# Second group's first load on the scalar queue, and other cuts of the first group's stores

## The chip, the cores and the metric

The kernel runs on one core of a Trainium2 chip. The metric is the device time of one execution in microseconds (us). The core has, among others, VectorE (DVE in the profile, does all the products here), ScalarE (ACT, two activations and some transfers) and SyncE (SP, only issues transfers). Data moves between HBM (the device's memory) and SBUF (the on-chip memory of 128 partitions) by 16 DMA engines. A transfer is issued by an engine's queue: those of SyncE are named q1 in the profile, those of ScalarE q10. Each transfer here covers 128 partitions, and its data go as one packet for each partition, so 8 packets on each of the 16 DMA engines.

## The reference

```python
def setup_inputs():
    batch, seq, hidden, n_experts, k = 16, 1024, 512, 8, 2
    ...
def reference(x, router_logits, k):
    logits_max = np.max(router_logits, axis=-1, keepdims=True)
    probs = np.exp(router_logits - logits_max)
    probs = probs / np.sum(probs, axis=-1, keepdims=True)
    topk_indices = np.argsort(probs, axis=-1)[..., -k:]
    topk_probs = np.take_along_axis(probs, topk_indices, axis=-1)
    topk_probs = topk_probs / np.sum(topk_probs, axis=-1, keepdims=True)
    x_expanded = x[:, :, np.newaxis, :].repeat(k, axis=2)
    return (x_expanded * topk_probs[..., np.newaxis]).astype(np.float32)
```

For each of 16,384 tokens (x is 16 x 1024 x 512, float32) the two largest of 8 router logits give two weights, and the token's 512 values are written twice, once times each weight. So 33.6 MB of x and 0.5 MB of logits are read, and 67.1 MB of output written.

## The kernel before, in words

Every partition holds 128 tokens, called rows here: 65 in a first group and 63 in a second (GROUPS). A row is 2 KB of x and 4 KB of output. The tile `xs` has room for 65 rows of x in each partition, and both groups use it; the second group's rows stand one place higher in it (BASE). The tile `osp` has room for L rows of output. Before that it serves as room for the logits and the steps of the search for the two largest (lines 14 to 38), which ends with two activations on ScalarE that leave the weights in `WA`.

For each group the kernel issues the loads of LOADS (line 120), 6, 28 and 31 rows in the first group and 16, 16 and 31 in the second, and then goes through the group's entries of STORES. An entry is (first row, number of rows, tile, place): VectorE multiplies these rows by their two weights (line 133) and puts the products into `osp`, or into `xs` itself over rows that are no longer needed (a product takes twice the room of its row), and then the store is issued (line 145). A product that writes again over `osp` from its start is made in two instructions (FREE): a few rows first, whose place was stored long ago, and the rest when the store of the place behind them has landed.

All transfers keep the program's order on their queue. All go over SyncE's queue, but for the very first store (3 rows), which goes over ScalarE's. A queue's transfers run one behind the other on the DMA engines. A load of the second group has to wait until the products that stand in its place in `xs` have been stored: the first 16 rows (places 1 to 16) for the first group's third store, out of places 0 to 31; the last 31 rows (places 33 to 63) for the fifth, out of places 33 to 64.

The order on SyncE is thus: load 6 rows, both parts of the logits, load 28, load 31; stores two to five of the first group; loads 16, 16 and 31 of the second; its four stores. In the text the stores of a group are counted with the one on ScalarE as the first.

Of the kernel before, what the change touches and what calls it, by code (L numbers as in the profile page):

```python
# [1 line left out]

# [4 lines left out]

F32 = mybir.dt.float32
ALU = mybir.AluOpType
ACTF = mybir.ActivationFunctionType  # L10
P = 128


def top2_weights(nc, WA, dlt, room, logits, E):

    tt = nc.vector.tensor_tensor
    hi, lo, n = None, None, E  # L20
    while n > 1:
        n //= 2
        if hi is None:
            a, b = logits[:, :, 0:n], logits[:, :, n : 2 * n]
            nhi, nlo = room(n), b
            tt(nhi, a, b, op=ALU.max)  # L26
            tt(nlo, a, b, op=ALU.min)  # L27
        else:
            a, b = hi[:, :, 0:n], hi[:, :, n : 2 * n]
            nhi, nlo, tmp = room(n), room(n), room(n)  # L30
            tt(tmp, lo[:, :, 0:n], lo[:, :, n : 2 * n], op=ALU.max)  # L31
            tt(nlo, a, b, op=ALU.min)  # L32
            tt(nlo, nlo, tmp, op=ALU.max)  # L33
            tt(nhi, a, b, op=ALU.max)  # L34
        hi, lo = nhi, nlo
    tt(dlt, hi[:, :, 0], lo[:, :, 0], op=ALU.subtract)  # L36
    nc.scalar.activation(WA[:, :, 0], dlt, ACTF.Sigmoid, scale=-1.0)  # L37
    nc.scalar.activation(WA[:, :, 1], dlt, ACTF.Sigmoid, scale=1.0)  # L38

GROUPS = [65, 63]

LOADS = [[6, 28, 31], [16, 16, 31]]
BASE = [0, 1]

STORES = [
    [(0, 3, "osp", 0), (3, 15, "osp", 3), (18, 16, "xs", 0), (34, 15, "osp", 0), (49, 16, "xs", 33)],
    [(0, 16, "osp", 2), (16, 16, "xs", 0), (32, 15, "osp", 0), (47, 16, "xs", 32)],
]  # L50

L = 18

FREE = [3, 2]


@with_exitstack
def kernel(
    ctx: ExitStack,
    tc: tile.TileContext,  # L60
    x: bass.AP,
    router_logits: bass.AP,
    k: bass.AP,
    out: bass.AP,
):
    nc = tc.nc
    B, S, D = x.shape
    E = router_logits.shape[-1]
    N = B * S
    assert int(k) == 2 and E == 8 and N == P * sum(GROUPS)  # L70
    M = N // P

    x_v, o_v, rl_v = [], [], []
    t0 = 0
    for n in GROUPS:
        t1 = t0 + P * n
        x_v.append(
            x.rearrange("b s d -> (b s) d")[t0:t1].rearrange("(p m) d -> p m d", p=P)
        )
        o_v.append(  # L80
            out.rearrange("b s k d -> (b s) k d")[t0:t1].rearrange(
                "(p m) k d -> p m k d", p=P
            )
        )
        rl_v.append(
            router_logits.rearrange("b s e -> (b s) e")[t0:t1].rearrange(
                "(p m) e -> p m e", p=P
            )
        )
        t0 = t1  # L90

    wpool = ctx.enter_context(tc.tile_pool(name="wpool", bufs=1))
    xs = wpool.tile([P, max(GROUPS), D], F32)
    osp = wpool.tile([P, L, 2, D], F32)
    WA = wpool.tile([P, M, 2], F32)
    dlt = wpool.tile([P, M], F32)


    flat = osp.rearrange("p l k d -> p (l k d)")
    taken = [0]  # L100

    def room(n):
        o = taken[0]
        taken[0] += M * n
        return flat[:, o : o + M * n].rearrange("p (m n) -> p m n", n=n)

    logits = room(E)

    def place(where, at, n):

        if where == "osp":
            return osp[:, at : at + n]
        return xs[:, at : at + 2 * n, :].rearrange("p (r k) d -> p r k d", k=2)

    m0 = 0
    for g, G in enumerate(GROUPS):
        x0, r = BASE[g], 0
        for n in LOADS[g]:
            tc.keep_in_program_order(
                nc.sync.dma_start(xs[:, x0 + r : x0 + r + n, :], x_v[g][:, r : r + n, :])  # L120
            )
            r += n
            if g == 0 and r == 6:
                n0 = GROUPS[0]
                tc.keep_in_program_order(nc.sync.dma_start(logits[:, :n0], rl_v[0]))  # L125
                tc.keep_in_program_order(nc.sync.dma_start(logits[:, n0:], rl_v[1]))  # L126
                top2_weights(nc, WA, dlt, room, logits, E)
        assert r == G
        for r, n, where, at in STORES[g]:
            og = place(where, at, n)  # L130
            again = where == "osp" and at == 0 and r > 0
            for a, b in [(0, FREE[g]), (FREE[g], n)] if again else [(0, n)]:
                nc.vector.tensor_tensor(  # L133
                    og[:, a:b],
                    xs[:, x0 + r + a : x0 + r + b, :]
                    .unsqueeze(2)
                    .to_broadcast([P, b - a, 2, D]),
                    WA[:, m0 + r + a : m0 + r + b, :]
                    .unsqueeze(3)
                    .to_broadcast([P, b - a, 2, D]),  # L140
                    op=ALU.mult,
                )

            queue = nc.scalar if g == r == 0 else nc.sync
            tc.keep_in_program_order(queue.dma_start(o_v[g][:, r : r + n], og))  # L145
        m0 += G


# [1 line left out]
_INS = ['x', 'router_logits', 'k']  # L150
_OUTS = [((16, 1024, 2, 512), 'float32')]

_NUMBERS = {'k': 2}


# [26 lines left out]
```

## Time and profile before

| | |
|---|---|
| median of 3 runs | 239.92 us (239.89 to 240.08) |
| profiled execution | 239.92 us, of which the profile's span is 238.1 us |
| VectorE busy | 141.9 us, 60% of the span |
| ScalarE busy | 1.8 us |
| moved by DMA | 101.19 MB, 425 GB/s over the span |
| products of 16 rows (128x16384) | 17.22 us each |
| product of 15 rows (128x15360) | 16.16 us |
| products of 13, 12, 3 and 2 rows | 14.03, 12.96, 3.35, 2.28 us |

The profile shows one execution. Its busy view cuts the span into 40 equal slices with a digit for the busy tenths of each; the DMA line there is the mean of 16 engines, and a long packet counts in the slice in which it begins, so that neighbouring digits go up and down. The queue view gives for each queue packets, megabytes and the share of 16 engines' time that the packets took. For a short window that share can exceed 100%, since packets that begin in the window count whole. The chain of waits goes back from the last instruction through whatever released each step; a transfer stands there from its issue to its landing, its wait in the queue included.

### The profile page before, as it was taken

The numbers are of one execution on the slowest core, as the hardware profiler recorded it, in microseconds if no ns is written. First come the engines' busy times: TensorE is split into PE (matmuls) and PEld (weight loads), VectorE is DVE, ScalarE is ACT, GpSimd is POOL, SyncE is SP. The second block draws the span as 40 slices with busy tenths as digits, with TensorE's granted clock in tenths as the row PEclk, the third lists the DMA queues.
The fourth block names the chain that finished last, engine by engine and source line by source line (L and its number), as shares of the span: only waits on it lengthen the run. The fifth ranks groups of instructions, "written<-read, shape, count | busy, mean of one in ns | idle before, by whom it ended". The sixth has DMA issues, their size and how long they took to land.

```text
span 238.1 us, 102 instructions
## 1 busy us (share of the span) xinstructions
DVE 141.9 (60%) x22; ACT 1.8 (1%) x3; POOL 0.2 (0%) x4
## 2 busy tenths in 40 slices
DVE  0650499999699999100000699999406999950000
ACT  2000000000000000000000000000000000000000
POOL 0000000000000000000000000000000000000000
DMA  7979998979999999989899999898989999989894
GB/s 265 550 337 500 430 418 374 506 330 495 429 429 407 473 423 402 495 352 528 352 440 435 435 446 501 352 495 374 506 374 462 418 407 451 475 351 517 352 528 176
DMA packets 2448, 101.19 MB, mean 425 GB/s; under 512 B 272, under 2 KB 400, under 8 KB 528
## 3 DMA queue, kind: packets, MB, share of 16 engines
q1 hardware_dynamic: 2304, 99.62, 97.2%
q10 hardware_dynamic: 144, 1.57, 1.5%
HBM read 34.08 MB, written 67.11 MB: 425 GB/s over the span
## 4 chain that ended last, share of the span: by engine, by line
DMA 48%; DVE 40%; SPq 1%; issue 0%; DVEq 0%
DMA xs<-in_x_dram 26%; DVE osp L133 25%; DMA out_dram<-osp 22%; DVE xs L133 14%; SPq L125 0%; SPq L126 0%; SPq L120 0%; SPq L145 0%; DVEq L133 0%
## 5 line engine op out<-in xcount | busy, mean ns | idle before, releaser
L133 DVE TENSOR_TENSOR osp<-xs,WA 128x3072 f32<-128x3072 f32 (+5 forms) x7 | 69.4, 9908 | 61.6 <-DMA xs<-in_x_dram 47.5
L133 DVE TENSOR_TENSOR xs<-xs,WA 128x16384 f32<-128x16384 f32 x4 | 68.9, 17224 | 0.1
L26 DVE TENSOR_TENSOR osp<-osp 128x512 f32<-128x512 f32 x1 | 0.7, 692 | 8.1 <-DMA osp<-in_router_logits_dram 8.1
L37 ACT ACT_TABLE_LOAD x1 | 1.3, 1283 | 0.7 <-PEq L163 0.7
L27 DVE TENSOR_TENSOR osp<-osp 128x512 f32<-128x512 f32 x1 | 0.7, 691 | 0.0
L34 DVE TENSOR_TENSOR osp<-osp 128x256 f32<-128x256 f32 (+1 forms) x2 | 0.7, 352 | 0.0
L32 DVE TENSOR_TENSOR osp<-osp 128x256 f32<-128x256 f32 (+1 forms) x2 | 0.7, 352 | 0.0
L31 DVE TENSOR_TENSOR osp<-osp 128x256 f32<-128x256 f32 (+1 forms) x2 | 0.7, 352 | 0.0
L33 DVE TENSOR_TENSOR osp<-osp 128x256 f32<-128x256 f32 (+1 forms) x2 | 0.7, 351 | 0.0
L37 ACT ACTIVATE WA<-dlt 128x128 f32<-128x128 f32 x1 | 0.3, 314 | 10.1 <-DVE dlt L36 10.1
L36 DVE TENSOR_TENSOR dlt<-osp 128x128 f32<-128x128 f32 x1 | 0.3, 291 | 0.0
L38 ACT ACTIVATE WA<-dlt 128x128 f32<-128x128 f32 x1 | 0.3, 298 | 0.0
L163 POOL MEMSET const-bfloat16-1.0<- 128x1 bf16 x1 | 0.1, 101 | 0.0
L163 POOL MEMSET const-uint8-127<- 128x1 uint8 x1 | 0.1, 101 | 0.0
L163 POOL MEMSET const-float32-0.0<- 128x1 f32 x1 | 0.1, 98 | 0.2 <-issue 0.2
L163 POOL MEMSET const-float32-1.0<- 128x1 f32 x1 | 0.1, 98 | 0.0
## 6 DMA issues: line engine op xcount, KB each, us to landing
out_dram<-osp SPq DMA_DIRECT2D x3, 7680.0 KB, 23.4
xs<-in_x_dram SPq DMA_DIRECT2D x2, 7936.0 KB, 41.7
xs<-in_x_dram SPq DMA_DIRECT2D x2, 4096.0 KB, 40.4
xs<-in_x_dram SPq DMA_DIRECT2D x1, 7168.0 KB, 24.8
xs<-in_x_dram SPq DMA_DIRECT2D x1, 1536.0 KB, 6.0
out_dram<-osp ACTq DMA_DIRECT2D x1, 1536.0 KB, 24.8
osp<-in_router_logits_dram SPq DMA_DIRECT2D x1, 260.0 KB, 6.2
osp<-in_router_logits_dram SPq DMA_DIRECT2D x1, 252.0 KB, 6.4
```

Of the source, the lines that this page charges most:

```text
L26: tt(nhi, a, b, op=ALU.max)
L27: tt(nlo, a, b, op=ALU.min)
L31: tt(tmp, lo[:, :, 0:n], lo[:, :, n : 2 * n], op=ALU.max)
L32: tt(nlo, a, b, op=ALU.min)
L33: tt(nlo, nlo, tmp, op=ALU.max)
L34: tt(nhi, a, b, op=ALU.max)
L36: tt(dlt, hi[:, :, 0], lo[:, :, 0], op=ALU.subtract)
L37: nc.scalar.activation(WA[:, :, 0], dlt, ACTF.Sigmoid, scale=-1.0)
L38: nc.scalar.activation(WA[:, :, 1], dlt, ACTF.Sigmoid, scale=1.0)
L133: nc.vector.tensor_tensor(og[:, a:b], xs[:, x0 + r + a : x0 + r + b, :] .unsqueeze(2) .to_broadcast([P, b - a, 2, D]), WA[:, m0 + r + a : ...
L163: nc = _bacc.Bacc("TRN2", target_bir_lowering=False, num_devices=1)
```

## The change

The first group's stores are cut to 3, 16, 16, 16 and 14 rows; they were 3, 15, 16, 15 and 16. `osp` gets 19 places for rows instead of 18. The second group's first load (16 rows) is issued by ScalarE's queue; it was SyncE's. An added dependency makes it wait until the first group's fourth store has landed. So it is issued while the fifth, now of 14 rows, is on SyncE's queue. The second group's middle load stays on SyncE's queue, directly behind that fifth store. Which engine makes which product, and in which order, is as before.

```diff
 STORES = [
-    [(0, 3, "osp", 0), (3, 15, "osp", 3), (18, 16, "xs", 0), (34, 15, "osp", 0), (49, 16, "xs", 33)],
+    [(0, 3, "osp", 0), (3, 16, "osp", 3), (19, 16, "xs", 0), (35, 16, "osp", 0), (51, 14, "xs", 37)],
     [(0, 16, "osp", 2), (16, 16, "xs", 0), (32, 15, "osp", 0), (47, 16, "xs", 32)],
 ]
 
-L = 18
+L = 19
...
     m0 = 0
+    stores = []
     for g, G in enumerate(GROUPS):
         x0, r = BASE[g], 0
         for n in LOADS[g]:
-            tc.keep_in_program_order(
-                nc.sync.dma_start(xs[:, x0 + r : x0 + r + n, :], x_v[g][:, r : r + n, :])
-            )
+
+            queue = nc.scalar if g == 1 and r == 0 else nc.sync
+            load = queue.dma_start(xs[:, x0 + r : x0 + r + n, :], x_v[g][:, r : r + n, :])
+            if queue is nc.scalar:
+                tc.add_manual_dep(
+                    load.ins,
+                    stores[-2].ins.name,
+                    mybir.DependencyInfo(
+                        mybir.DependencyClass.Sync, mybir.DependencyReason.DATA
+                    ),
+                    reason="begin when the store ahead of the last has landed",
+                )
+            tc.keep_in_program_order(load)
             r += n
...
             queue = nc.scalar if g == r == 0 else nc.sync
-            tc.keep_in_program_order(queue.dma_start(o_v[g][:, r : r + n], og))
+            stores.append(queue.dma_start(o_v[g][:, r : r + n], og))
+            tc.keep_in_program_order(stores[-1])
         m0 += G
```

## Prediction, made before the changed kernel was run

> **What bounds the kernel now.** I read the busy slices first, then the DMA queues, the chain of waits, and the transfers one by one by window. Busy slices and queues:
>
> ```profile
> DVE  0650499999699999100000699999406999950000
> DMA  7979998979999999989899999898989999989894
> ...
> HBM read 34.08 MB, written 67.11 MB: 425 GB/s over the span
> ...
> q1 hardware_dynamic: 2304, 99.62, 97.2%
> q10 hardware_dynamic: 144, 1.57, 1.5%
> ```
>
> VectorE has idle stretches of many slices; the DMA engines have none. q1 is SyncE's queue, q10 ScalarE's: their packets fill 97.2% + 1.5% = 98.7% of 16 engines over 238.1 us, 235.0 us each. The 3.1 us left are the head (0.72 us to the first issue, about 1 us more to its first packets) and the tail behind the last packets. So I look only for what makes a DMA engine idle or slow. The chain agrees, if one knows that a transfer's time in it includes its wait in the queue:
>
> ```profile
> by line: DMA xs<-in_x_dram 25.5%; DVE osp L133 25.4%; DMA out_dram<-osp 22.4%; DVE xs L133 14.5%; issue 0.2%; SPq L125 0.2%; SPq L126 0.2%; SPq L120 0.2%; SPq L145 0.1%; DVEq L133 0.0%
> ...
> 43.09 22.91 DMA out_dram<-osp
> ...
> 96.66 36.05 DMA xs<-in_x_dram
> ...
> 150.05 30.49 DMA out_dram<-osp
> ```
>
> The store issued at 43.09 lands at 66.00, but the load ahead of it on SyncE landed only at 47.85 (issued 2.60, 45.3 us to landing): its own data took 18.15 us for 7.86 MB, 433 GB/s. With issue plus time to landing from the DMA view, every later transfer begins where the one ahead ends. Landings: first group's stores 2 to 5 at 66.0, 85.3, 103.4, 123.0; second group's loads at 132.7, 142.4, 161.2; its stores at 180.5, 199.8, 218.0, 237.3. A 16-row store takes 19.3 us (66.0 to 85.3), a 16-row load 9.7 us (132.7 to 142.4). No stretch is empty.
>
> What two queues cost when they run together, the scalar queue's first store shows (issued at 16.00, between two SyncE loads). The DMA views of four windows: 7.70 to 17.72 (before it), 17.72 to 18.25 (just behind the issue), 23.12 to 23.60 (its second row has gone out) and 26.56 to 29.35 (well in), with packets, MB and share of 16 engines:
>
> ```profile
> q1 hardware_dynamic: 64, 3.67, 84.5%
> ...
> q1 hardware_dynamic: 16, 0.92, 433.2%
> ...
> q1 hardware_dynamic: 16, 0.92, 522.3%
> ...
> q1 hardware_dynamic: 16, 1.02, 83.9%
> q10 hardware_dynamic: 16, 0.20, 16.5%
> ```
>
> A share times 16 engines times the window, by packets, is one packet's time (it may end behind the window). Alone, a 57,344-byte load packet takes 0.845 x 16 x 10.02 / 64 = 2.12 us. The one that began between 17.72 and 18.25 (433.2% of 0.53 us) took 2.30 us, 0.18 more; the one begun at 23.1, the last of its load, 2.51 us, 0.39 more. After that both queues go in turn, one packet of each, and fill 83.9% + 16.5% = 100.4%: no loss and no gain by the alternation.
>
> **The change, part by part.** The profiled execution took 239.92 us, the median of the three runs; its span is 238.13, so 1.79 lie outside. The sum is made against 239.92.
>
> 1. *Bytes and packets.* Five stores and three loads a group, as before; the cuts move rows from one store to another. 15-row and 16-row stores run at 433 and 434 GB/s (18.15 us for 7.86 MB; 19.34 for 8.39). Cost 0.
>
> 2. *The second store has 16 rows.* VectorE makes it in 17.23 us (128x16384 row) instead of 16.16, from 26.91 to 44.15: the issue is 1.07 us later. Cover: the load that lands at 47.85, whose last packets end on the first engine at 47.1. An issue needs time to its first packets: 1.0 us at the start (issue 0.72, packets from 1.7), at most 4.1 us for the scalar store (issue 16.00, its first packets at 20.1, after those already running). With 1.0 it is ready at 45.2, and the cost is 0; with 4.1 at 48.2, and the engines idle 1.1 us. I take 0: the 4.1 contain packets of 2.1 us that were running.
>
> 3. *The third to fifth stores.* VectorE: third product 44.15 to 61.4; then 3 rows (3.35) to 64.7; the other 13 of the fourth wait for the second store's landing, 47.85 + 19.3 = 67.2 (before: 66.0), and take 14.03 (128x13312 row) to 81.2; the last, 14 rows, 17.22 x 14/16 = 15.1, to 96.3. The store ahead of each ends at 67.2, 86.5 and 105.9, so the issues at 61.4, 81.2 and 96.3 are 5 to 10 us ahead of need (before: 5.6, 6.3, 7.2). Cost 0.
>
> 4. *The load on ScalarE's queue.* One issue (0.37 us in the scalar row at 16.00) moves from SyncE to ScalarE, with a wait until the fourth store has landed, 105.9. Behind it on ScalarE stands nothing; its activations end at 12.6. SyncE loses one issue of about 1 us (at 96.66); its next, the load of rows 16 to 31, now stands behind the last store and keeps that queue full. From about 107 to 110 on, packets of store (56 KB, 2.12 us) and load (32 KB, 1.21 us, the 9.7 us by 8) go in turn. Together they need 16.9 + 9.7 = 26.6 us from 105.9: 132.5, and one or two rows of the next load slip in between, so the load lands at 133.5 to 135 instead of 132.7; the store at 129 to 130 instead of 123.0.
>
>    The Trainium skill, page "DMA: Bandwidth & Descriptors", section "Queues, rings and completion order", says that an engine drains a whole packet, typically 9 to 17 descriptors, before it turns to another ring. By that, if each row were one descriptor, the load's 8 rows per engine would go in one piece and land near 119. The trace turns after each row (16 and 16 packets in the last window), so 133.5 to 135 stands; the sum is the same by both.
>
> 5. *What waits for these.* VectorE's first product of the second group starts about 1.5 us later, at 134.3; its store is issued at 151.5, needed at 161.2. The second product ends at 168.8, needed at 180.5. From there the products wait for that landing at 180.5 again, so the lag is gone. The last load waits for the last store's landing (now 129.5), and SyncE issues nothing meanwhile that is wanted before; its engines have the middle load until 142.4. Cost 0.
>
> 6. *Two queues at once.* The cost is the stretching seen above. Upper end: both stretches again, 0.18 + 0.39 = 0.57 us on each engine. Lower end: below zero. At 124.7, just after the issue at 123.05, two engines have a packet of 1.40 and 1.56 instead of 1.21 us; the two engines that finish last do so 0.3 us behind the rest (completions at 237.22 and 237.28, the others to 236.94). If the moved issue spares this, -0.3. I take +0.3: the row at 17.7 is the nearest, a scalar transfer entering a busy queue, and it put the latest engine back by 0.2; to this I add a quarter of the second stretch, which stood at the last packet of a load with a store behind it. Here it is a store's last packet with a load behind it, and at 122 that turn cost nothing (the load behind it took its plain 9.7 us).
>
> Sum: 239.92 + 0 + 0 + 0 + 0 + 0 + 0.3 = 240.2 us.
>
> **Rivals.**
>
> *A. Forecast: the stream stays full, and the second queue costs 0 to 0.45 us.* 239.9 to 240.4, most likely 240.2.
>
> *B. The stretches come in full or more than once.* For: both stood in the only place of this trace where two queues run. Against: the six further turns there cost nothing. 0.57 gives 240.5; twice that, 241.1.
>
> *C. The second store comes too late.* SyncE's queue runs dry at 47.1 to 47.5. It decides if issue to first packet exceeds 47.1 - 44.15 = 3.0 us; the trace leaves 1.0 to 4.1. At 4.1 the whole stream behind it shifts by 1.1: 241.0. Against: the start's 1.0 us.
>
> *D. Turns between large store and load packets cost each time.* The load's 8 packets make 16 turns; at 0.18 each, 2.9 us: 242.8. For: both streams are large here, while the scalar packets of before were 12 KB. Against: the 100.4%.
>
> *E. It gets faster.* There is 3.1 us beside the stream, in head and tail, and the change touches neither. The late engines give 0.3 (239.6); to exceed 0.2% another 0.2 must come from stretches at the other turns, or from a load and a store running at once in one engine. Against the last: in turns the packets lasted 2.34 and 0.46 us, 100.4% of the time.
>
> **How the numbers follow.** A measurement of this kernel can tell about 0.2%, 0.48 us, from no change: 239.44 to 240.40 is "same". Chances: A 0.46, B 0.28, C 0.08, D 0.06, E 0.12 (half of it beyond 0.2%). Slower: B + C + D = 0.42; same: A and half of E, 0.52; faster 0.06. The range for 8 in 10 leaves out D, half of C, the far end of B and the far half of E: 239.6 to 241.0. The likeliest case alone has 239.9 to 240.4.
>
> **What will show it.** The DMA slices still full, both queues together at 98 to 99% of the engines; the second group's first load landing at 133.5 to 135, the fifth store at about 129.5; the first product of the second group later and VectorE's last start unchanged but for the stretch. C shows as a wider gap than 19.4 us between 47.9 and the second store's landing; B and D as shares over 100% by packet in the windows from 106 to 132, with all later landings shifted alike. The prediction is wrong if landings behind 142 shift by more than 1 us, or come earlier by more than 0.4.

## The result and the profile after

The changed kernel takes 240.49 us (median of 12, 240.28 to 241.19); before, in the same sessions, 239.89 (12 runs). The ratio is 1.0025 with a 95% interval of 1.0018 to 1.0033: slower by 0.25%, 0.6 us. The profiled execution took 240.39 us with a span of 238.6, so its 0.47 us over the profiled one of before stand for most of the change, not for all.

The page after, busy slices and queues (q1 SyncE's, q10 ScalarE's; packets, MB, share of 16 engines):

```profile
DVE  0650499399999999300000299999806999950000
DMA  7979998989898999998999998999898989899894
...
q1 hardware_dynamic: 2160, 95.42, 93.2%
q10 hardware_dynamic: 288, 5.77, 5.7%
HBM read 34.08 MB, written 67.11 MB: 424 GB/s over the span
```

The stream is as full as before: 98.9% of the engines' time against 98.7%. But the same 101.19 MB take longer. From the chain after:

```profile
2.75 45.08 DMA xs<-in_x_dram
...
82.39 23.45 DMA out_dram<-osp
...
105.91 29.66 DMA xs<-in_x_dram
...
152.91 28.11 DMA out_dram<-osp
```

Start plus duration are landings: 47.83 for the first group's last load (before: 47.85), 105.84 for the fourth store, 135.57 for the load on ScalarE's queue, 181.02 for the second group's first store (before: 180.54). So the first half has lost nothing: the fourth store landed at 103.4 before, with two rows fewer sent by then, and a row of output takes 1.2 us (19.34 by 16). The loss lies behind 105.84, and the stores at the end run as before.

Where it lies, single packets show. In a short window in which one packet begins on each of 16 engines, share times window is the mean time of a packet. Before, in windows 44.75 to 45.3 (last packets of the 31-row load, ahead of the second store), 119.55 to 120.05 (last packets of the fifth store, ahead of the second group's loads) and 157.7 to 158.5 (last packets of the second group's last load, ahead of its first store):

```profile
q1 hardware_dynamic: 16, 1.02, 436.4%
...
q1 hardware_dynamic: 16, 1.05, 483.6%
...
q1 hardware_dynamic: 16, 1.02, 302.9%
```

These are 2.40, 2.42 and 2.42 us, where such packets take 2.34, 2.42 and 2.34 elsewhere: stretches of 0.06, 0.00 and 0.08 us at the three turns between loads and stores. I call them the first, second and third turn. After, the windows are 44.7 to 45.3 (first turn), 109.2 to 109.75 (the fifth store's third packet, just before the scalar load's first), 111.7 to 112.4 (that load's first packets), 115.39 to 118.7 (one packet of each) and 158.3 to 158.9 (third turn):

```profile
q1 hardware_dynamic: 16, 1.02, 390.3%
...
q1 hardware_dynamic: 16, 0.92, 482.1%
...
q10 hardware_dynamic: 16, 0.52, 200.9%
...
q1 hardware_dynamic: 16, 0.92, 64.0%
q10 hardware_dynamic: 16, 0.52, 36.6%
...
q1 hardware_dynamic: 16, 1.02, 430.7%
```

The first turn costs nothing (2.34 us). At the load's entry, where its packets first come between those of the store, a store packet takes 2.65 instead of 2.12 us, 0.53 more, and the load's first packet 1.41 instead of 1.21, 0.19 more. Then the two queues take turns, packet by packet, and fill 64.0% + 36.6% = 100.6%, without loss. The third turn costs 2.58 - 2.34 = 0.24. All stretches behind 8 us add up to 1.48 us on the mean engine, against 0.75 before (of which the scalar store's entry at 17 to 26 us has 0.48 after and 0.58 before). That is 0.73 more. The last landing is only 0.47 later (237.75 against 237.28), because the two engines that finished 0.3 us behind the others before are not behind after.

VectorE has a wait that I had not foreseen, in the waits after:

```profile
DVE xs L144 <- DMA xs<-in_x_dram: 3.8, 1, 3.8
```

The third product now takes rows 19 to 34, and row 34 comes with the last load, landed at 47.83. Its store is issued at 65.18, not at 61.4.

### The profile page after: what moved, and what is told of

Read it like the earlier page. It is cut to its first block, busy times and chain, and to the rows that moved or that the text cites. A ratio compares the mean times of both kernels' runs of the same rounds, so it can differ in the third digit from the quotient of the medians.

```text
span 238.6 us, 104 instructions
## 1 busy us (share of the span) xinstructions
DVE 141.8 (59%) x22; ACT 1.8 (1%) x3; POOL 0.2 (0%) x4
## 2 busy tenths in 40 slices
DMA packets 2448, 101.19 MB, mean 424 GB/s; under 512 B 272, under 2 KB 400, under 8 KB 528
## 4 chain that ended last, share of the span: by engine, by line
DMA 53%; DVE 35%; SPq 1%; issue 0%; DVEq 0%; ACTq 0%
DMA xs<-in_x_dram 31%; DMA out_dram<-osp 22%; DVE osp L144 20%; DVE xs L144 14%; SPq L122 0%; SPq L136 0%; SPq L137 0%; DVEq L144 0%; ACTq L122 0%
## 5 line engine op out<-in xcount | busy, mean ns | idle before, releaser
L144 DVE TENSOR_TENSOR osp<-xs,WA 128x3072 f32<-128x3072 f32 (+3 forms) x7 | 71.4, 10213 | 58.3 <-DMA xs<-in_x_dram 49.0
L144 DVE TENSOR_TENSOR xs<-xs,WA 128x16384 f32<-128x16384 f32 (+1 forms) x4 | 66.8, 16692 | 3.9 <-DMA xs<-in_x_dram 3.8
```

What stands on the lines that cost most here:

```text
L144: nc.vector.tensor_tensor(og[:, a:b], xs[:, x0 + r + a : x0 + r + b, :] .unsqueeze(2) .to_broadcast([P, b - a, 2, D]), WA[:, m0 + r + a : ...
```

## The experiments

The theory at the start: the second queue's entry at 109 us is the cost. Rival: the cuts cost it, through the late third product.

**Each half of the change alone.** First the cuts, with the load on SyncE's queue:

```diff
-    [(0, 3, "osp", 0), (3, 15, "osp", 3), (18, 16, "xs", 0), (34, 15, "osp", 0), (49, 16, "xs", 33)],
+    [(0, 3, "osp", 0), (3, 16, "osp", 3), (19, 16, "xs", 0), (35, 16, "osp", 0), (51, 14, "xs", 37)],
-L = 18
+L = 19
```

> The changed cuts (3, 16, 16, 16, 14) alone, all loads on SyncE's queue as before. Theory (the cost is the second queue's entry at 109 us, where the profile after shows the store's packets stretched by 0.54 us and the first load packets by 0.19): as before, 239.9 +- 0.15 us. Rival (the cuts cost it: the third product now needs row 34 and so waits for the third load at 47.9, and its store is issued at 65.2, only 1.2 us before the queue runs dry): 240.4 to 240.6 here.

Measured: 241.00 us (before 239.86), ratio 1.0049 (1.0037 to 1.0061). Then the changed kernel with the cuts of before:

```diff
-    [(0, 3, "osp", 0), (3, 16, "osp", 3), (19, 16, "xs", 0), (35, 16, "osp", 0), (51, 14, "xs", 37)],
+    [(0, 3, "osp", 0), (3, 15, "osp", 3), (18, 16, "xs", 0), (34, 15, "osp", 0), (49, 16, "xs", 33)],
-L = 19
+L = 18
```

> The cuts of before (3, 15, 16, 15, 16), and only the second group's first load on ScalarE's queue when the fourth store has landed. Theory of the second queue's entry: 240.5 +- 0.2 us, with stretched packets 3 to 6 us after the scalar issue and the landings behind them 0.4 to 0.7 us late. Rival (the cuts): 239.9.

Measured: 241.39 us, ratio 1.0070 (1.0049 to 1.0090). Both halves cost more alone (1.1 and 1.5 us) than together (0.6), so neither theory stands as it was put. The cuts alone, in windows 119.85 to 120.3 (second turn) and 158.2 to 158.7 (third):

```profile
q1 hardware_dynamic: 16, 0.92, 579.9%
...
q1 hardware_dynamic: 16, 1.02, 645.3%
```

That is 2.61 instead of 2.12 us and 3.23 instead of 2.34: 0.49 and 0.89 us, with no second queue near. Before, the same two turns cost 0.00 and 0.08, and the transfers at the third turn are the same in both kernels. The late third product is not the place: its store lands 19.33 us behind the second one's landing (67.17 to 86.50), the 19.34 of before.

The queue alone has little stretch on the mean, but on single engines. Windows 107.73 to 107.77 (two of the packets beside which the load enters) and 158.6 to 158.8 (the last two to begin the third turn):

```profile
q1 hardware_dynamic: 2, 0.13, 961.1%
...
q1 hardware_dynamic: 2, 0.13, 214.2%
```

They take 3.08 us instead of 2.42, and 3.43 instead of 2.34. The last store's completions (one for each engine) come between 236.66 and 238.68 us, where the spread before is 0.66. The two engines that fell behind at 108 stayed behind, and the slowest one sets the end.

**No second queue for the first store.**

```diff
-            queue = nc.scalar if g == r == 0 else nc.sync
+            queue = nc.sync
```

> The kernel before with its very first store (3 rows) on SyncE's queue too, so that no second queue is ever used. If a second queue's entry costs time whatever it carries, the two stretches in the profile before (0.18 us at 17.7, 0.39 at 23.1, each on all engines) go: 239.3 to 239.5 us. If these have another cause (the first writes to HBM, or a load's end before a store), the time stays at 239.9, and a stretch shows at the new turn from load to store at about 47 us.

Measured: 240.28 us, ratio 1.0016 (1.0008 to 1.0025). The stretches at 17 and 23 us go, as the theory has it; the time does not fall, because the first turn now costs 1.19 us (its lines stand below, beside the run that takes this cost away). The second and third cost nothing.

**The load enters beside a load.**

```diff
-                    stores[-2].ins.name,
+                    stores[-1].ins.name,
```

> The changed kernel, but the scalar load waits for the fifth store's landing instead of the fourth's, so that it enters beside a load (the second group's middle one) and not beside a store. If the entry as such costs: the same 0.5 to 0.7 us, 240.5. If the cost comes from a load entering while a store runs: 239.9 to 240.1. Its landing will be near 143 us and the first product's store is issued near 160, still ahead of need at 161, so that the later start costs at most a few tenths.

Measured: 247.45 us, ratio 1.0315 (1.0302 to 1.0328): my expectation of the load's landing was wrong. The load goes in turn with the packets of the 31-row load too and lands at 149.8, not 143; VectorE's lines:

```profile
149.88 17.23 DVE L144 TENSOR_TENSOR osp<-xs,WA 128x16384 f32<-128x16384 f32 x1 [52.34 <-DMA xs<-in_x_dram]
167.13 0.34 SPq L156 DMA_DIRECT2D out_dram<-osp  x1
```

The last load lands at 161.5, and with no store issued before 167.1 the engines stand idle; that store lands at 187.9, 7.1 us later than 161.5 + 19.3. This is what the prediction's cover for VectorE's later start (10 us of other transfers) is worth when it is gone. It says nothing on the entry.

**Is it the last store's packet size, or the load's wait?** A second theory was that 56 KB packets at the turn are dear. The cuts again, with the 14 rows in the fourth store:

```diff
-    [(0, 3, "osp", 0), (3, 16, "osp", 3), (19, 16, "xs", 0), (35, 16, "osp", 0), (51, 14, "xs", 37)],
+    [(0, 3, "osp", 0), (3, 16, "osp", 3), (19, 16, "xs", 0), (35, 14, "osp", 0), (49, 16, "xs", 33)],
```

> Cuts of 3, 16, 16, 14 and 16 rows, all loads on SyncE's queue: like the run of the cuts alone, with the 14-row store ahead of the last instead of last, so that the third product is as late as there and the packet at the turn from stores to loads is 64 KB as before. Theory now (a turn between stores and loads stretches the packets at it; with 56 KB packets at the turn near 120 us it cost 0.5 us twice, with 64 KB packets under 0.1 three times): no stretch at 120 to 123, 239.9 to 240.4 according to what the turn near 158 costs. Rival (the late third product or its tight issue costs): 240.9 to 241.1 as in that run.

Measured: 241.06 us, ratio 1.0050 (1.0037 to 1.0064). The second turn, now with 64 KB packets, costs 0.61 and the third 0.73. So the packet size is not it. The entry beside 64 KB packets, by an earlier issue:

```diff
-                    stores[-2].ins.name,
+                    stores[-3].ins.name,
```

> The changed kernel with the scalar load waiting for the third store's landing (86.5) instead of the fourth's, so that it enters beside the 16-row store's 64 KB packets. If the entry costs by the packets beside which it falls (56 KB stretched, 64 KB hardly): stretch below 0.15 us near 90 and 239.9 to 240.3. If any entry of a load beside a store costs 0.5 to 0.7: 240.4 to 240.6. If single engines fall out of turn, as in the run with the scalar load alone: up to 241.5, with the last landings spread by 1 to 2 us.

Measured: 243.29 us, ratio 1.0140 (1.0126 to 1.0154). Engines fall far out of turn: the fourth store's completions spread from 113.4 to 117.8, the last one's from 237.6 to 240.5. And the load's moment of issue on one queue, with the changed cuts and with those of before:

```diff
-            queue = nc.scalar if g == 1 and r == 0 else nc.sync
+            queue = nc.sync
...
-            if queue is nc.scalar:
+            if g == 1 and r == 0:
```

> The changed cuts with the second group's first load on SyncE's queue, but issued only when the fourth store has landed (105.9), as the changed kernel does on ScalarE's: one queue, and the load is queued 17 us before its turn instead of 25, with an idle queue of issues behind it. Theory L (a turn is dear when the transfer behind it has long been queued): the stretch near 120 falls from 0.58 us to under 0.2, and the time to 240.2 to 240.7 according to the turn near 158. Rival (these cuts make the turns dear by themselves): 240.9 to 241.2 as without the dependency.

> The kernel before with the same dependency: its first load of the second group is issued on SyncE's queue when the fourth store has landed (103.5). Both theories: the turn near 122 cost only 0.03 us before and can hardly fall; 239.7 to 240.0. If it goes up by 0.5 or more, the cost of a turn hangs on the moment of the issue in some other way than by its length in the queue.

Measured: 241.07 us, ratio 1.0044 (1.0031 to 1.0058), and 239.96, ratio 0.9999 (0.9990 to 1.0008). The load's moment changes neither; the turns cost 0.42 and 0.96 in the first, nothing and 0.06 in the second, as without the wait.

**The first store on SyncE's queue, early or late.** The next runs change what stands at the first turn. First, the first store behind the second on SyncE's queue:

```diff
+    held = []
...
-            queue = nc.scalar if g == r == 0 else nc.sync
-            tc.keep_in_program_order(queue.dma_start(o_v[g][:, r : r + n], og))
+            held.append((o_v[g][:, r : r + n], og))
+            if g == r == 0:
+                continue
+            while held:
+                tc.keep_in_program_order(nc.sync.dma_start(*held.pop()))
```

> The kernel before with its first store (3 rows) on SyncE's queue behind the second store, so that no second queue is used and the turn from the third load goes to 60 KB packets as before, not to 12 KB ones (that turn cost 1.19 us where the first store stood first). Theory (second queue's entry and turns are all that stretches the stream): the stretches at 17 and 23 us, 0.58 together, are gone, the turn at 45 costs 0 to 0.2: 239.2 to 239.6. Rival (the turn from the third load costs 1 us or more without a second queue whatever follows): 240.2 or more.

Measured: 242.16 us, ratio 1.0097 (1.0083 to 1.0111). The three turns, windows 40.3 to 41.2, 118.6 to 120.4 and 157.4 to 160.4:

```profile
q1 hardware_dynamic: 16, 1.02, 261.2%
...
q1 hardware_dynamic: 16, 1.05, 163.6%
...
q1 hardware_dynamic: 16, 1.02, 104.3%
```

Both sides missed: the first turn costs 0.01, but the later ones have come back, 0.53 and 0.79 on the mean, and some engines end 2.5 us behind. Next, the kernel of the run without a scalar store, with the first store's issue alone held back from 16.0 to 41.1 us:

```diff
-                nc.vector.tensor_tensor(
+                product = nc.vector.tensor_tensor(
...
+            if g == r == 0:
+                held = (o_v[g][:, r : r + n], og)
+                continue
+            if held:
+                first = nc.sync.dma_start(*held)
+                tc.add_manual_dep(
+                    first.ins,
+                    product.ins.name,
...
+                    reason="begin when the second product is made",
+                )
+                tc.keep_in_program_order(first)
+                held = None
-            queue = nc.scalar if g == r == 0 else nc.sync
+            queue = nc.sync
```

> The kernel before with its first store on SyncE's queue, ahead of the second as in the run without a scalar store, but issued only when the second product is made (41.2 instead of 16.0). Theory L: the stretch of 1.19 us at the turn from the third load to these 12 KB packets falls under 0.2, and if the later turns are as cheap as there (0.02 together), 239.1 to 239.4, faster than before; if they are as dear as in the run with the first store behind the second, 239.8 to 241. Rival (12 KB packets behind a load are dear in themselves): the stretch stays over 0.8, 240.2 or more.

Measured: 242.19 us, ratio 1.0091 (1.0078 to 1.0105). The pair differs in nothing but that moment (the second store's issue moves by 0.3 us with it). Issued at 15.96, windows 40.4 to 41.2, 119.8 to 120.7 and 158.0 to 158.9, the three turns:

```profile
q1 hardware_dynamic: 16, 1.02, 441.7%
...
q1 hardware_dynamic: 16, 1.05, 268.7%
...
q1 hardware_dynamic: 16, 1.02, 261.3%
```

Issued at 41.06, windows 40.4 to 41.2, 118.8 to 120.4 and 157.4 to 160.3:

```profile
q1 hardware_dynamic: 16, 1.02, 293.2%
...
q1 hardware_dynamic: 16, 1.05, 187.6%
...
q1 hardware_dynamic: 16, 1.02, 104.5%
```

Early: 3.53, 2.42 and 2.35 us, stretches of 1.19, 0.00 and 0.01. Late: 2.35, 3.00 and 3.03, stretches of 0.00, 0.58 and 0.69, and the last completions spread from 237.1 to 239.5, where early they spread from 236.9 to 237.6. The moment of one issue, long before, moves the cost from the first turn to the later ones. It hardly changes the sum on the mean engine (1.20 and 1.27 us); most of the 1.9 us between the two runs is the spread, since the last engine sets the end. The last two kernels are the changed one, its load on ScalarE's queue, with the first store on SyncE's, early and late. Early:

```diff
-            queue = nc.scalar if g == r == 0 else nc.sync
+            queue = nc.sync
```

> The changed kernel with its very first store on SyncE's queue too, so that the load is the only transfer on ScalarE's. Theory: the stretches at 17 and 23 us go (0.47), the turn from the third load to the 12 KB packets costs about 1.2 as in the run without a scalar store, the entry at 109 stays at 0.7: 240.8 to 241.1. If the entry at 109 costs more because ScalarE's queue had been used before, it falls and the time is 240.2 to 240.5.

Late, by the same lines as the late first store above:

```diff
+            if g == r == 0:
+                held = (o_v[g][:, r : r + n], og)
+                continue
...
-            queue = nc.scalar if g == r == 0 else nc.sync
+            queue = nc.sync
```

> The changed kernel with the first store on SyncE's queue, issued only when the second product is made: the load is then the only transfer on ScalarE's queue, as in the run with the scalar load only, where its entry cost 0.01 us on the mean and set single engines back by up to 1.3. Theory L: the 1.12 us at the third load's turn go, 239.4 to 240.0. Rival: 240.5 or more.

Measured: 240.56 us, ratio 1.0027 (1.0015 to 1.0038), and 243.06, ratio 1.0128 (1.0114 to 1.0141). Early, the first turn costs 1.12, the load's entry 0.01 and the third turn 0.09. Late, they cost 0.00, 1.2 and 0.48, and the slowest engine is 2.7 us behind the fastest. My expectation, that the late issue only takes away the first turn's cost, was wrong in the same way.

**What the runs say together.** Take the lead of the first store on SyncE's queue over the moment when the last packets of the first group's last load begin:

| kernels | lead, us | first turn | second turn, or the scalar load's entry | third turn |
|---|---|---|---|---|
| before; before with late load; queue alone | 1.7 | 0.06, 0.09, 0.17 | 0.00, 0.01, 0.08 | 0.08, 0.06, 0.21 |
| no scalar store; scalar load only | 24 | 1.19, 1.12 | 0.00, 0.01 | 0.01, 0.09 |
| after | 0.6 | 0.00 | 0.73 | 0.24 |
| cuts alone; 14 rows in the fourth; cuts with late load | 0.5 to 0.6 | 0.00 | 0.4 to 0.6 | 0.7 to 1.0 |
| first store behind the second; first store late; the latter with scalar load | -0.6, -0.6, -1.7 | 0.00 to 0.01 | 0.5 to 1.2 | 0.79, 0.69, 0.48 |

(All in us on the mean engine. For the scalar load's entry, the load's first packets are counted too; in the second turn they are not, and add up to 0.2. Left out are the load beside a load and the entry beside 64 KB packets; their second turns cost 0.5 and more too, and the idle time and the disorder there leave no third turn to compare.) With a lead of 1.7 us or more the first turn costs something and the later ones at most 0.21; with 0.6 or less the first turn costs nothing, the second turn or the entry 0.4 or more, and the third 0.24 or more. In these kernels the line falls somewhere between 0.6 and 1.7 us. The change crosses it, since its second store has 16 rows. Two rivals do not order the table: the first packets behind the load are of 60 KB in the kernel before and in the run with the first store behind the second, on either side of the line; and ScalarE's queue had been used before the load in the run of the queue alone, where the mean entry cost 0.08, and not in the last run, where it cost 1.2. The table speaks of the mean engine only: the queue alone has cheap turns there and still loses 1.5 us, most of it because two engines finish late. The timelines of before and after:

```profile
43.09 0.35 SPq L145 DMA_DIRECT2D out_dram<-osp  x1
```

```profile
44.14 0.35 SPq L156 DMA_DIRECT2D out_dram<-osp  x1
```

with the packets in question beginning at 44.8 before and 44.7 after. That the moment of the issue can have such an effect is shown by the pair, at leads of 24 and -0.6 us. That it is the second store's delay, and not another part of the cuts, that moves the changed kernel into the dear group is inferred from the table: a run of the kernel before with only that issue held back by 1 us was not made. Why a turn that costs nothing leaves dear ones behind, what the engines carry over for 75 us, and why the scalar queue together with the cuts makes the third turn cheaper (0.24 against 0.9) and keeps the engines together, where the same queue alone drives them apart, is open. No version was faster than the kernel before.

## Why the prediction was right or wrong

The forecast of 240.2 us had the right sign, the range held 240.49, and the largest new stretch, 0.73 us, stands at the load's entry, where step 6 looked for it. The landings behind 142 came about 0.5 us later, less than the 1 us that would have spoken against it. The time is what rival B, with a chance of 0.28, gave for the stretches in full (240.5), just outside the forecast's own range (239.9 to 240.4); the change comes out a little beyond the 0.2% that divided "same" from "slower".

- Step 1, bytes and packets: right, the stores of 14 to 16 rows run at the same rate.
- Step 2, the second store: right that it is not late for the stream. It was issued at 44.14 and landed at 67.19, 19.35 behind the load. Rival C is refuted: no wider gap. But "cost 0" looked only at the engines running dry. By the table, the 1.07 us may be what brings on the dear turns behind it; that is inferred, not shown.
- Step 3: the third product's issue at 61.4 was wrong, because row 34 comes only with the last load, which the step left out. The issue came at 65.18, while the second store's packets ended from 66.4 on. There the cover was 1.2 us, not 5, and it still held: that store landed at 86.51, 19.32 behind.
- Step 4: landings of 133.5 to 135 and 129 to 130 were forecast; 135.57 and 130.72 came. They are late by the entry's 0.73. The turn after each row held: 64.0% and 36.6% in the window. So the Trainium skill's typical packet of 9 to 17 descriptors (page "DMA: Bandwidth & Descriptors", section "Queues, rings and completion order") does not describe these rows, if a row is one descriptor; by the estimate made from it the load would have landed near 119.
- Step 5: right. The second group's first store was issued at 152.91 (151.5 forecast) and needed at 161.7; VectorE's wait for that store's landing falls from 11.1 to 8.7 us and takes up the lag.
- Step 6, the term that was too small: 0.18 for the entry and a quarter of the second stretch were put in, 0.3. The entry cost 0.73, and the third turn rose by 0.16, which no step had. Against it, the lower end's guess came true that the two late engines would be spared: the stretches grew by 0.73 on the mean engine, the last landing came only 0.47 later.
- Rival D, a cost at each of the 16 turns, is refuted by the 100.6%. Rival E's overlap too.

The reason given for the cost, "the second queue", does not stand by itself. The queue alone costs 1.5 us, mostly by two late engines; the cuts alone, which the prediction put at 0, cost 1.1 us by the turns, and the two together 0.6. That the sum came within 0.3 us of the measurement without these parts is luck.

## What to carry to other kernels

In a kernel whose DMA engines are always full, busy share cannot tell a good stream from a bad one: look at the time of single packets at each turn between loads and stores, and at the spread of a transfer's completions over the engines, since the last engine sets the end. An issue that is early enough to leave no gap may still change the stream far behind it, so a cut that delays an issue by 1 us is worth a run of its own. Test the halves of such a change apart before naming a cause: here they did not add.

## What the runs showed of the hardware that I had not expected

- A packet at a turn between loads and stores took from 0 to 1.2 us longer on the mean engine; the same 31-row load packets at the third turn took 2.35 to 3.3 us. In one pair of runs the stretch there went from 0.01 to 0.69 us by the moment of one issue, over 100 us before.
- Under load, a store issued at 65.18 had its first packets at 66.4 with no gap ahead of them: at most 1.2 us from issue to data were needed. The scalar load, on a queue of its own, had its first packet 5.9 us after its issue (105.91 to 111.8): two packets of the other queue went ahead of it, and the second was stretched.
- Two queues in turn lost nothing (100.4% and 100.6%); what can cost is the entry (0.01 to 1.2 us on the mean engine), and engines that drop out of turn with the rest: 0.66 us in one packet and 1.1 in another on two engines put the last landing 2 us behind the first.
